# A fused decoder layer: TensorE's instructions in the written order, attention in whole score steps with projections drawn between

## The chip, the cores and the metric

The kernel runs on one core of a Trainium2 chip. The core has five engines that run side by side and wait for each other by semaphores: TensorE (PE; its weight loads are listed apart as PEld), VectorE (DVE), ScalarE (ACT), GpSimd (POOL) and SyncE (SP), which only issues DMAs. The metric is the device time of one execution in microseconds, the median of three runs.

## The reference

One layer of a decoder on 512 positions of width 1024, all in float32:

```
h = rms_norm(x, g_mix);  qa,ka,va,qb,kb,vb,gates = split(h @ w_in)        # 8 + 8 heads of 64
qa, ka = rope(qa), rope(ka)
ya = moba_attention(qa, ka, va)            # softmax over own block of 256 and past blocks, causal
yb = stick_breaking_attention(qb, kb, vb)  # a = sigmoid(z) * prod of (1 - sigmoid(z)) of later keys, causal
g  = sigmoid(gates + b_gate)
x  = x + (g[0] * (ya @ w_branch_a) + g[1] * (yb @ w_branch_b)) @ w_out
h  = rms_norm(x, g_ffn);  u = causal_depthwise_conv(h @ w_up)             # width 3
x  = x + (silu(u_gate) * u_val) @ w_down                                  # d_ff 2816
return rms_norm(x, g_final)
```

With 512 positions and blocks of 256 the three chosen past blocks are all there are, so the MoBA part is plain causal softmax attention.

## The kernel before

All matrix products are made in three passes (`mm3`, line 70): each operand is split into a high and a low half (`whi`, `wlo` for weights, two planes of one tile for activations), and high x high, high x low and low x high are summed in PSUM. A projection is 8 such triples over the depth of 1024 ("8 units" below), 24 TensorE instructions of 512 columns. A weight block of 128 x 1024 is loaded by SP (`raw`, 512 KB), its high half made by ScalarE (line 66) and its low half by VectorE (line 67); three such blocks are held (`wsp`), so a block's halves are made when the block three before is used up.

In the order of the program: the input is loaded transposed in 8 pieces `xk`, scaled by the norm's weight and split (`xg`), while the Q and K columns of the first two pairs of MoBA heads (`qk0`, lines 182 to 185) are summed over them and the sum of squares `ssq` is gathered. `rstd_cols` (line 113) sums `ssq` over the partitions by products with `ones` (line 116) and takes the reciprocal root, `bcast_rows` (line 132) spreads it over the partitions by TensorE transposes (line 135) into `rb`. Then V of the MoBA heads (`vproj_a`), then attention. `moba_half` makes Q or K of a pair: a copy `pc`, its rotated half `sw` by four DMAs on ScalarE's queue, three VectorE products, a split. `sb_qk` makes those of the stick-breaking heads (`o`, then the split), `vproj_b` their V, in products of 256 columns.

`attend(branch, pairs)` (line 331) handles two pairs of heads at a time, in three units of query tiles of 128: tiles 0 and 1, tile 2, tile 3. For each unit: scores into PSUM tile `sc` (two buffers, `psc`), for MoBA with a mask product in front (line 281); the weights (`weights_a`: maximum, exponential, reciprocal, product; `weights_b`: two sigmoids, selects on GpSimd, scans on VectorE, product); transposes of the weights into PSUM tile `tp` (one buffer, `ptr`); the copy `aT` out of it, by VectorE for some MoBA units and by ScalarE for the rest. Then the products with V into `tp` (line 358). Projections use PSUM tile `mm` (two buffers).

After attention come the gates, the two output projections and their sum, `w_out`, a second norm (`norm2`, line 463, with `ssq2`), up-projection with convolution and gate, down-projection and the last norm.

The program is written in this order, but the order on each engine is set by a list scheduler with a model of its own (line 610). It takes what it thinks is ready: so, before, projections are pulled into attention wherever the model sees a gap, `mm` triples are split between scores, and products of later stages run ahead of a waiting one. `tc.issue_after` (line 352) only holds the products with V behind the last transposes.

Of the kernel before, what the change touches and what calls it, by code (L numbers as in the profile page):

```python
# [25 lines left out]
NG = 3  # L26
NWARM = 8
LAST = 4
# [10 lines left out]
def trunk_layer(ctx: ExitStack, tc: tile.TileContext, xT: bass.AP, w: bass.AP, vec: bass.AP,  # L39
# [3 lines left out]
    def pool(stack, name, bufs, space=None, side=None):  # L43
# [40 lines left out]

    warmb = consts.tile([128, 512], BF, name="warmb")
    nc.vector.memset(warmb, 0.0)
# [53 lines left out]

    hlp = pool(asta, "hlp", 2)
    st1 = ExitStack()
# [6 lines left out]
    for _ in range(NWARM):  # L149
        nc.tensor.matmul(warm, warmb[:, :128], warmb, start=True, stop=True)  # L150
    xks = {}
# [36 lines left out]
    def vproj_a():  # L188
        ps = [pool_.tile([128, S], F32, name=n) for pool_, n in ((pmm, "mm"), (pmm, "mm"), (p1, "v0"), (p1, "v1"))]
        for k in range(KT):  # L190
            if k % 2 == 0:
                wt = wload(("va", k // 2))
            for t in range(QT):
                a = (xg[k][:, 0, t * 128:(t + 1) * 128], xg[k][:, 1, t * 128:(t + 1) * 128])
                mm3(ps[t], a, blk(wt, k % 2, 512), k == 0, k == KT - 1)
        for t in range(QT):
            if t % 2:
                nc.scalar.activation(va[:, t], ps[t], AF.Copy, scale=r1[:, t:t + 1])
            else:
                nc.vector.tensor_scalar(va[:, t], ps[t], r1[:, t:t + 1], None, op0=OP.mult)  # L200

    def vproj_b(g):
        wt = tuple(wload(("vb", g, h)) for h in range(2))
        for t in range(QT):
# [3 lines left out]
            for k in range(KT):  # L208
                a = (xg[k][:, 0, t * 128:(t + 1) * 128], xg[k][:, 1, t * 128:(t + 1) * 128])
                mm3(o, a, blk(wt[k // 4], k % 4, 256), k == 0, k == KT - 1)  # L210
            if t % 2:
# [4 lines left out]
    mst = ExitStack()  # L216
    mp = pool(mst, "mp", 1, side="right")
    va = mp.tile([128, QT, 512], F32, name="va")
    rt = pool(mst, "rt", 2, side="right")
    mqkp = pool(mst, "mqkp", 4, side="right")  # L220
    swp = pool(mst, "swp", 2, side="right")
    tg = mp.tile([128, 2, S], F32, name="tg")
    nc.sync.dma_start(tg, trig)
    for i in range(2):
        nc.vector.tensor_mul(tg[:, i], tg[:, i], rb)

    def proj(wt):
        ps = pmm.tile([128, S], F32, name="mm")
        for k in range(KT):
            mm3(ps, blk(wt, k), (xg[k][:, 0], xg[k][:, 1]), k == 0, k == KT - 1)  # L230
        return ps

# [24 lines left out]
    def moba_qk(p):  # L257
        for n in range(2):
            moba_half(p, n, proj(wload(("mqk", p, n))), swp)

    def sb_qk(p):
        sc = {}
        for n, nm in enumerate(("q", "k")):
            ps = proj(wload(("sqk", p, n)))
# [5 lines left out]
            sc[nm] = sqkp.tile([128, 2, S], F32R, name=f"hl{nm}")  # L270
            split_out(sc[nm], o)
        stk["b", p] = [(sc["q"], sc["k"], h * 64) for h in range(2)]

    UNITS = ((0, 1), (2,), (3,))

    def scores(br, p, seg):
        sc = psc.tile([128, 2, 512], F32, name="sc")
        if br == "a":
            for j, (qt, o, n) in enumerate(seg):
                for h in range(2):  # L280
                    nc.tensor.matmul(sc[:, h, o + n - 128:o + n], identb, maskb, start=j == 0, stop=False,
                                     skip_group_check=True)
        for qt, o, n in seg:
            for m, (c, d) in enumerate(((0, 0), (0, 1), (1, 0))):
                for h in range(2):
                    q, k, r0 = stk[br, p][h]
                    nc.tensor.matmul(sc[:, h, o:o + n], q[r0:r0 + 64, c, qt * 128:(qt + 1) * 128],  # L287
                                     k[r0:r0 + 64, d, :n], start=br == "b" and m == 0, stop=m == 2,
                                     skip_group_check=True)
        return sc  # L290

# [38 lines left out]

    def attend(br, pairs):
        v = va if br == "a" else vb
        aT = {p: atp.tile([128, 2, 10 * 128], F32, name="aT") for p in pairs}
        for u, qts in enumerate(UNITS):
            seg = []
            for qt in qts:
                seg.append((qt, sum(s[2] for s in seg), (qt + 1) * 128))
            W = seg[-1][1] + seg[-1][2]
            scs = [scores(br, p, seg) for p in pairs]
            ws = [(weights_a if br == "a" else weights_b)(sc, seg) for sc in scs]  # L340
            for p, a in zip(pairs, ws):
                tp = ptr.tile([128, 2, 512], F32, name="tp")
                for h in range(2):
                    for c in range(0, W, 128):
                        last = nc.tensor.transpose(tp[:, h, c:c + 128], a[:, h, c:c + 128], ident)  # L345
                o = seg[0][0] * (seg[0][0] + 1) // 2 * 128
                if br == "b" or u % 2:
                    nc.scalar.activation(aT[p][:, :, o:o + W], tp[:, :, :W], AF.Copy)
                else:
                    nc.vector.tensor_copy(aT[p][:, :, o:o + W], tp[:, :, :W])  # L350
        av = ptr.tile([128, 2, 512], F32, name="tp")
        with tc.issue_after(last.ins):
            for j, p in enumerate(pairs):
                for qt in range(QT):
                    o = qt * (qt + 1) // 2 * 128
                    for kb in range(qt + 1):
                        for h in range(2):
                            nc.tensor.matmul(av[h * 64:(h + 1) * 64, j, qt * 128:(qt + 1) * 128],  # L358
                                             v[:, kb, (2 * p + h) * 64:(2 * p + h + 1) * 64],
                                             aT[p][:, h, o + kb * 128:o + (kb + 1) * 128],  # L360
                                             start=(kb == 0), stop=(kb == qt))
        for j, p in enumerate(pairs):
# [12 lines left out]
    ptr = pool(psA, "ptr", 1, PSUM)  # L375
    attend("a", (0, 1))
    moba_qk(2)
    moba_qk(3)
    attend("a", (2, 3))
# [4 lines left out]
    sqkp = pool(ysta, "sqkp", 4, side="right")  # L384
    gsig = pool(ysta, "gsig", 6, side="right")
    sb_qk(0)
    sb_qk(1)
    vproj_b(0)
    attend("b", (0, 1))
    sb_qk(2)  # L390
    sb_qk(3)
    vproj_b(1)
    attend("b", (2, 3))

    def gate(i, b):
        ps = proj(wload(("g", i, b)))
        g = gsig.tile([128, S], F32, name="g")
        nc.vector.tensor_mul(g, ps, rb)
        return g

    pend = {}

    def gates(i):
        pend[i] = []
        for b in range(2):
            g = gate(i, b)
            nc.scalar.activation(g, g, AF.Sigmoid, bias=bgate[:, b * 8 + i:b * 8 + i + 1])
            pend[i].append(g)

    gates(0)  # L410
    for i in range(1, NG):
        gates(i)
    psA.close()
# [14 lines left out]
    for i in range(KT):  # L428
        if i >= NG:
            gates(i)  # L430
        wab = wload(("ab", i))
# [182 lines left out]
```

## Time and profile before

| | us |
|---|---|
| median of three runs | 755.24 (755.08 to 755.56) |
| the profiled execution | 755.25 |
| its span, first to last instruction | 752.9 |
| TensorE busy | 742.3 (99%) |
| TensorE weight loads busy | 612.8 (81%) |
| VectorE busy | 446.9 (59%) |
| ScalarE busy | 309.6 (41%) |

The span is what the trace shows; 2.35 us of the execution lie around it. Matrix products overlap by their pipeline, so their single durations (0.39 us for 512 columns) add up to more than the time that they take; the time is read from start to start. The granted clock says which share of full speed TensorE had in a stretch.

### The profile page before, as it was taken

To read this page: it belongs to the slowest core of one execution; us is meant where nothing else is said; L and a number is where in the kernel's file an instruction comes from. 1 tells how busy PE (TensorE), PEld (TensorE's weight loads), DVE (VectorE), ACT (ScalarE), POOL (GpSimd) and SP (SyncE) were. 2 spreads that over 40 slices of the span, in tenths; PEclk is the share of its full clock that TensorE was granted. 3 is DMA by queue.
4 is the path that set the end of the run, shared out by engine and by line. 5 is a ranking of instruction groups with operands and counts; after the bars stand their busy time and mean duration, and the time that the engine had idled before them with its cause. 6 is when DMAs were issued, how large, how long until landed. Compare 5 with 4: busy or idle time off the path is not lost.

```text
span 752.9 us, 9484 instructions
## 1 busy us (share of the span) xinstructions
PE 742.3 (99%) x3792; PEld 612.8 (81%) x3792; DVE 446.9 (59%) x638; ACT 309.6 (41%) x445; POOL 20.4 (3%) x40
## 2 busy tenths in 40 slices
PE   9999998999999999999999999999999999999996
PEld 6887787979878888888888888888888888888885
DVE  6588767684883544446548777767777673122233
ACT  6445526363563323324345444444443442121233
POOL 0000000220310000000000000000000000000000
PEclk9999999999999999999999999999999999999999
DMA  9542211111123423232322323232322223323202
GB/s 311 153 129 84 84 58 57 51 62 57 57 85 123 158 85 111 84 111 85 112 84 84 112 84 112 85 110 86 104 92 95 103 89 108 111 85 102 94 28 111
DMA packets 23899, 74.11 MB, mean 98 GB/s; under 512 B 2992, under 2 KB 3632, under 8 KB 23856
## 3 DMA queue, kind: packets, MB, share of 16 engines
q1 hardware_dynamic: 21456, 70.11, 28.5%
q10 hardware_dynamic: 2400, 3.41, 1.6%
q8 instruction: 29, 0.48, 0.3%
q14 instruction: 14, 0.11, 0.0%
HBM read 69.31 MB, written 2.10 MB: 95 GB/s over the span
## 4 chain that ended last, share of the span: by engine, by line
PE 97%; DVE 1%; DMA 0%; ACT 0%; issue 0%; ACTq 0%
PE mm L71 23%; PE mm L73 23%; PE mm L72 23%; PE d L73 5%; PE d L72 5%; PE d L71 5%; PE q L184 3%; PE sc L287 3%; PE tp L358 2%; PE tp L345 2%; PE v L72 0%; PE v L71 0%; PE v L73 0%; DMA raw<-w 0%; PE d L517 0%; DVE st L296 0%
## 5 line engine op out<-in xcount | busy, mean ns | idle before, releaser
L66 ACT ACTIVATE whi<-raw 128x1024 fp32r<-128x1024 f32 (+2 forms) x128 | 129.8, 1020 | 244.3 <-PE mm L72 88.8
L67 DVE TENSOR_TENSOR wlo<-raw,whi 128x1024 fp32r<-128x1024 f32 (+2 forms) x128 | 149.5, 1173 | 98.7 <-ACT whi L66 97.6
L73 PE MATMUL mm<-h,wlo 128*128 128x512 f32 x352 | 137.1, 390 | 0.0
L72 PE MATMUL mm<-h,whi 128*128 128x512 f32 x352 | 137.0, 389 | 0.0
L71 PE MATMUL mm<-h,whi 128*128 128x512 f32 x352 | 136.9, 389 | 0.0
L71 PE MATMUL mm<-xg,whi 128*128 128x512 f32 x224 | 88.3, 394 | 0.0
L73 PE MATMUL mm<-xg,wlo 128*128 128x512 f32 x224 | 88.2, 394 | 0.0
L72 PE MATMUL mm<-xg,whi 128*128 128x512 f32 x224 | 88.0, 393 | 0.0
L73 PEld LDWEIGHTS mm<-h,wlo 128*128 128x128 f32 x352 | 66.1, 188 | 13.8
L72 PEld LDWEIGHTS mm<-h,whi 128*128 128x128 f32 x352 | 66.1, 188 | 13.7
L71 PEld LDWEIGHTS mm<-h,whi 128*128 128x128 f32 x352 | 66.1, 188 | 13.6
L71 PE MATMUL d<-whi,gT 128*128 128x512 f32 x176 | 68.9, 393 | 0.0
L73 PE MATMUL d<-whi,gT 128*128 128x512 f32 x176 | 68.3, 389 | 0.0
L72 PE MATMUL d<-wlo,gT 128*128 128x512 f32 x176 | 68.3, 389 | 0.0
L490 DVE TENSOR_TENSOR u<-mm,rb 128x512 f32<-128x512 f32 x44 | 30.1, 688 | 37.8 <-PE mm L73 37.7
L71 PEld LDWEIGHTS mm<-xg,whi 128*128 128x128 f32 x224 | 42.1, 188 | 10.4 <-issue 1.7
L73 PEld LDWEIGHTS mm<-xg,wlo 128*128 128x128 f32 x224 | 42.1, 188 | 9.9 <-issue 1.5
L72 PEld LDWEIGHTS mm<-xg,whi 128*128 128x128 f32 x224 | 42.1, 188 | 9.2 <-issue 0.7
L73 PEld LDWEIGHTS d<-whi,gT 128*128 128x128 f32 x176 | 33.0, 188 | 6.8
L72 PEld LDWEIGHTS d<-wlo,gT 128*128 128x128 f32 x176 | 33.1, 188 | 6.6
L71 PEld LDWEIGHTS d<-whi,gT 128*128 128x128 f32 x176 | 33.1, 188 | 6.6
L234 ACT ACTIVATE gT<-t 128x512 fp32r<-128x512 f32 x22 | 13.9, 631 | 55.1 <-DVE t L499 55.1
(184 smaller groups left out, 1047.1 us busy)
## 6 DMA issues: line engine op xcount, KB each, us to landing
raw<-w SPq DMA_DIRECT2D x118, 512.0 KB, 3.3
xk<-xT SPq DMA_DIRECT2D x8, 256.5 KB, 5.3
sw<-pc ACTq DMA_DIRECT2D x32, 64.0 KB, 2.0
x1T<-xT SPq DMA_DIRECT2D x8, 256.0 KB, 5.1
raw<-w SPq DMA_DIRECT2D x6, 256.0 KB, 6.1
out<-on ACTq DMA_DIRECT2D x4, 256.0 KB, 2.7
out<-on SPq DMA_DIRECT2D x4, 256.0 KB, 2.5
tg<-trig SPq DMA_DIRECT2D x1, 512.0 KB, 7.5
```

The costliest lines, as they stand in the source:

```text
L66: nc.scalar.activation(hi[:, sl], raw[:, sl], AF.Copy)
L67: nc.vector.tensor_sub(lo[:, sl], raw[:, sl], hi[:, sl].bitcast(F32))
L71: nc.tensor.matmul(ps, a[0], b[0], start=start, stop=False)
L72: nc.tensor.matmul(ps, a[0], b[1], start=False, stop=False)
L73: nc.tensor.matmul(ps, a[1], b[0], start=False, stop=stop)
L184: nc.tensor.matmul(qk0[c], w0[i][:, (k % 2) * 512 + c * 128:(k % 2) * 512 + (c + 1) * 128], xg[k][:, j], start=(k == 0 and n == 0), stop=( ...
L234: nc.scalar.activation(hl[:, 0], o, AF.Copy)
L287: nc.tensor.matmul(sc[:, h, o:o + n], q[r0:r0 + 64, c, qt * 128:(qt + 1) * 128], k[r0:r0 + 64, d, :n], start=br == "b" and m == 0, stop=m ...
L345: last = nc.tensor.transpose(tp[:, h, c:c + 128], a[:, h, c:c + 128], ident)
L358: nc.tensor.matmul(av[h * 64:(h + 1) * 64, j, qt * 128:(qt + 1) * 128], v[:, kb, (2 * p + h) * 64:(2 * p + h + 1) * 64], aT[p][:, h, o + k ...
L490: nc.vector.tensor_mul(u, ps, rb2)
```

## The change

A line at the top makes TensorE's order that of the program text; the other engines are still ordered by the scheduler. Since nothing is pulled ahead on TensorE now, the text says what stands between the steps of attention. Projections become generators that yield after each triple (1.0 unit, or 0.5 for a triple of 256 columns) and stand in a list `fillers` in the order in which they are needed: Q and K of MoBA pairs 2 and 3, then of stick-breaking pairs 0 and 1, V, and so on to the gates. `attend` is written in steps: scores of unit 0 for both pairs, of unit 1 for both, transposes of unit 0 for the first pair, for the second, scores of unit 2, then the transposes of units 1 and 2, pair by pair. After each step `fill(gap)` draws as many units from the list as `GAPS_*` says. Of the scores, the mask products of both pairs stand first.

```diff
-NWARM = 8
+NWARM = 32
+    ctx.enter_context(tc.manual_schedule(engines={mybir.EngineType.PE}))
-            (eng if eng is not None and i < 2 else nc.sync).dma_start(raw[:, sl], w[WIDX[key]][:, sl])
-            if eng is not None and i == 1:
+            (eng if eng is not None and i == 0 else nc.sync).dma_start(raw[:, sl], w[WIDX[key]][:, sl])
+            if eng is not None and i == 0:
...
-    warmb = consts.tile([128, 512], BF, name="warmb")
+    warmb = consts.tile([128, 128], BF, name="warmb")
...
+    def proj(key, use):
+        wt = wload(key)
+        ps = pmm.tile([128, S], F32, name="mm")
+        for k in range(KT):
+            mm3(ps, blk(wt, k), (xg[k][:, 0], xg[k][:, 1]), k == 0, k == KT - 1)
+            if k < KT - 1:
+                yield 1.0
+        use(ps)
+        yield 1.0
...
+    def fill(n):
+        while n > 0 and fillers:
+            try:
+                n -= next(fillers[0])
+            except StopIteration:
+                fillers.pop(0)
...
-            scs = [scores(br, p, seg) for p in pairs]
-            ws = [(weights_a if br == "a" else weights_b)(sc, seg) for sc in scs]
-            for p, a in zip(pairs, ws):
...
+        steps = [(score, 0), (score, 1)] + [(turn, 0, p) for p in pairs] + [(score, 2)]
+        steps += [(turn, u, p) for u in (1, 2) for p in pairs]
+        for (f, *args), gap in zip(steps, gaps):
+            f(*args)
+            fill(gap)
...
+    fillers = [moba_qk(2), moba_qk(3), sb_qk(0), sb_qk(1), vproj_b(0), sb_qk(2), sb_qk(3), vproj_b(1)]
+    fillers += [gates(i) for i in range(NG)]
+    GAPS_A = (14, 0, 4, 6, 0, 4, 8, 4, 4)
+    GAPS_A2 = (10, 0, 3, 6, 0, 3, 6, 3, 3)
+    GAPS_B = (8, 4, 4, 4, 4, 4, 8, 4, 4)
+    attend("a", (0, 1), GAPS_A)
+    attend("a", (2, 3), GAPS_A2)
...
+    attend("b", (0, 1), GAPS_B)
+    attend("b", (2, 3), GAPS_B)
+    fill(1000)
```

Besides, the stick-breaking Q and K now share the four buffers of the MoBA ones, `vproj_a` takes its PSUM tiles in another order, the first weight block comes with one quarter on ScalarE's queue in place of two, and the warm-up is 32 products of 128 columns in place of 8 of 512.

The order on TensorE in the first MoBA attend, where `sc_651` and `sc_660` are the scores of unit 1 of the two pairs, `tp_635` the transposes of unit 0 of the first pair, and `mm_896` a projection. Before:

```order
L73 MATMUL mm_896<-xg1_99,wlo_892 128x512
...
L287 MATMUL sc_651<-hl1_399,hl0_385 128x384
L345 MATMUL tp_635<-ident_67,a1_610 128x128
L287 MATMUL sc_651<-hl1_399,hl0_385 128x384
L345 MATMUL tp_635<-ident_67,a1_610 128x128 x5
L287 MATMUL sc_651<-hl1_399,hl0_385 128x384 x4
...
L287 MATMUL sc_660<-hl1_427,hl0_413 128x384 x6
L71 MATMUL mm_896<-xg2_100,whi_891 128x512
```

After, with `sc_731` and `sc_732`, `tp_765` and `tp_806` in these places and `mm_712` and `mm_799` for the projections:

```order
L74 MATMUL mm_712<-xg5_105,wlo_708 128x512
...
L307 MATMUL sc_731<-hl1_425,hl0_411 128x384 x6
L307 MATMUL sc_732<-hl1_453,hl0_439 128x384 x6
L375 MATMUL tp_765<-ident_69,a1_636 128x128 x6
L72 MATMUL mm_712<-xg6_106,whi_707 128x512
...
L74 MATMUL mm_799<-xg1_101,wlo_795 128x512
L375 MATMUL tp_806<-ident_69,a1_649 128x128 x6
```

The scores of both pairs stand together, then the first pair's transposes whole, then four triples, then the second pair's.

The order on TensorE at the second norm, where `ssq` is the sum of squares, `n2r` the reciprocal root and the `mm` rows up-projections. Before:

```order
L72 MATMUL mm<-h_3131,whi 128x512
L116 MATMUL tp<-ones,ssq_3136 128x2 x4
L73 MATMUL mm<-h_3131,wlo 128x512
...
L72 MATMUL mm<-h_3133,whi 128x512
L135 MATMUL tp<-ident,n2r 128x128 x4
```

After:

```order
L73 MATMUL mm<-h_3157,whi 128x512
L74 MATMUL mm<-h_3157,wlo 128x512
L117 MATMUL tp<-ones,ssq_3158 128x2 x4
L136 MATMUL tp<-ident,n2r 128x128 x4
L72 MATMUL mm<-h_3150,whi 128x512
```

Before, 30 products stand between the two; now none.

The order on ScalarE in the first stick-breaking attend, where `a1` and `a2` are the two sigmoids of a score tile, `aT` the copies of transposes, and `hlq` (now `hl0`) the split of a projection's result `o`. Before:

```order
L312 ACTIVATE a1_1582<-sc_1568 128x2x384
L66 ACTIVATE whi_1838<-raw_1837 128x1024
L348 ACTIVATE aT_1482<-tp_1552 128x2x384
L314 ACTIVATE a2_1584<-sc_1568 128x2x384
L234 ACTIVATE hlq_1762<-o_1760 128x512
```

After:

```order
L332 ACTIVATE a1_1626<-sc_1600 128x2x384
L67 ACTIVATE whi_1787<-raw_1786 128x1024
L249 ACTIVATE hl0_1647<-o_1645 128x512
L334 ACTIVATE a2_1615<-sc_1599 128x2x384
L378 ACTIVATE aT_1490<-tp_1663 128x2x384
```

The first copy of transposes, `aT_1482` before and `aT_1490` now, has moved behind the split of a projection.

## Rows read from the trace of the kernel before

**Rows 1.** The page, parts 1 and 4: engines' busy time, and the chain's shares.

```profile
PE 742.3 (99%) x3792; PEld 612.8 (81%) x3792; DVE 446.9 (59%) x638; ACT 309.6 (41%) x445; POOL 20.4 (3%) x40
...
PE 97%; DVE 1%; DMA 0%; ACT 0%; issue 0%; ACTq 0%
```

**Rows 2.** Table of stretches: length, busy us (instructions) by engine, clock, DMA.

```profile
core 0: us, PE busy (x) PEld busy (x) DVE busy (x) ACT busy (x) POOL busy (x), PEclk, DMA share, GB/s
56.30:240.50 184.20, 181.54 (x1303) 150.60 (x1302) 124.79 (x198) 91.64 (x160) 19.31 (x32) 0.99 0.22 69
116.00:129.00 13.00, 10.34 (x70) 8.08 (x69) 11.91 (x23) 10.96 (x24) 0.00 (x0) 0.87 0.13 42
400.00:500.00 100.00, 100.00 (x443) 82.81 (x442) 76.93 (x100) 49.28 (x61) 0.00 (x0) 1.00 0.29 95
```

**Rows 3.** Timeline of TensorE, 116 to 130: start, length, line, names [idle before, releaser].

```profile
118.00 0.88 PE L345 MATMUL tp<-ident,a 128*128 128x128 f32 x6 [0.81 <-DVE aT L350]
...
123.07 0.88 PE L345 MATMUL tp<-ident,a 128*128 128x128 f32 x6 [0.90 <-ACT aT L348]
```

**Rows 4.** Chain of waits in order of time: start, length, what (instructions).

```profile
57.95 0.88 PE sc L287 x12
...
65.32 0.37 PE sc L287
...
67.01 0.55 PE sc L287 x4
...
84.39 0.65 PE tp L345 x6
...
109.22 0.72 PE sc L287 x6
...
145.35 1.41 PE sc L287 x18
...
192.63 1.58 PE sc L287 x24
```

**Rows 5.** Timeline of all engines, 0 to 40.

```profile
4.22 0.49 DVE L170 TENSOR_SCALAR xg<-xk 128x512 fp32r<-128x512 f32 x1 [2.25 <-DMA xk<-xT]
...
4.89 1.43 PE L184 MATMUL q<-xg,whi 128*128 128x512 f32 x4
...
5.41 1.43 DVE L67 TENSOR_TENSOR wlo<-raw,whi 128x256 fp32r<-128x256 f32 x4
...
24.41 1.48 DVE L159 TENSOR_TENSOR ssq<-ssq,sq 128x512 f32<-128x512 f32 x2
...
29.31 0.95 PE L116 MATMUL mm<-ones,ssq 128*128 128x2 f32 x8
```

**Rows 6.** Timeline of all engines, 389 to 399, the second norm.

```profile
389.71 1.06 ACT L66 ACTIVATE whi<-raw 128x1024 fp32r<-128x1024 f32 x1 [5.51 <-PE mm L72]
...
389.97 0.95 PE L116 MATMUL tp<-ones,ssq 128*128 128x2 f32 x8
...
390.79 1.28 ACT L123 ACT_TABLE_LOAD   x1
...
390.81 1.23 DVE L67 TENSOR_TENSOR wlo<-raw,whi 128x1024 fp32r<-128x1024 f32 x1 [5.21 <-ACT whi L66]
...
392.14 0.21 ACT L123 ACTIVATE n2s<-n2v 128x4 f32<-128x4 f32 x1
...
392.98 0.16 DVE L129 SCALAR_TENSOR_TENSOR n2r<-n2t,n2r 128x4 f32<-128x4 f32 x1
```

**Rows 7.** Timeline of VectorE, 60 to 160.

```profile
69.24 1.81 DVE L296 TENSOR_REDUCE st<-sc 128x2 f32<-128x768 f32 x2
...
74.74 0.95 DVE L350 COPY aT<-tp 128x768 f32<-128x768 f32 x1
...
81.46 0.69 DVE L249 TENSOR_TENSOR sw<-sw,tg 128x512 f32<-128x512 f32 x1 [2.18 <-DMA sw<-pc]
...
148.59 2.48 DVE L326 TENSOR_TENSOR_SCAN R<-a 128x128 f32<-128x128 f32 x4
...
151.91 1.79 DVE L326 TENSOR_TENSOR_SCAN R<-a 128x384 f32<-128x384 f32 x2
```

More of the change, by code (lines that the diff above doesn't have):

```diff
@@ L149, in trunk_layer @@
     for _ in range(NWARM):
-        nc.tensor.matmul(warm, warmb[:, :128], warmb, start=True, stop=True)
+        nc.tensor.matmul(warm[:, :128], warmb, warmb, start=True, stop=True)
     xks = {}
@@ L200, in vproj_a @@
                 nc.vector.tensor_scalar(va[:, t], ps[t], r1[:, t:t + 1], None, op0=OP.mult)
+    mqkp = pool(ysta, "mqkp", 4, side="right")
+    hlp = pool(ysta, "hlp", 2, side="right")
+    mst = ExitStack()
+    mp = pool(mst, "mp", 1, side="right")
+    va = mp.tile([128, QT, 512], F32, name="va")
+    rt = pool(mst, "rt", 2, side="right")
+    swp = pool(mst, "swp", 2, side="right")
+    tg = mp.tile([128, 2, S], F32, name="tg")
+    nc.sync.dma_start(tg, trig)
+    for i in range(2):
+        nc.vector.tensor_mul(tg[:, i], tg[:, i], rb)
+    def proj(key, use):
[7 more added lines that the diff above has]
+        yield 1.0
     def vproj_b(g):
@@ L214, in vproj_b @@
                 nc.vector.tensor_scalar(dst[:, 1], o, r1[:, t:t + 1], None, op0=OP.mult)
[L216 to L231, printed above, removed]
+            yield 0.5
+    def fill(n):
[4 more added lines that the diff above has]
+                fillers.pop(0)
     def split_out(hl, o):
@@ L269, in sb_qk, with scores @@
                 nc.vector.tensor_mul(o, ps, rb)
-            sc[nm] = sqkp.tile([128, 2, S], F32R, name=f"hl{nm}")
+            sc[nm] = mqkp.tile([128, 2, S], F32R, name=f"hl{n}")
             split_out(sc[nm], o)
+        for n, nm in enumerate(("q", "k")):
+            yield from proj(("sqk", p, n), lambda ps: use(n, nm, ps))
         stk["b", p] = [(sc["q"], sc["k"], h * 64) for h in range(2)]
     UNITS = ((0, 1), (2,), (3,))
-    def scores(br, p, seg):
-        sc = psc.tile([128, 2, 512], F32, name="sc")
+    def scores(br, pairs, seg):
+        scs = [psc.tile([128, 2, 512], F32, name="sc") for _ in pairs]
         if br == "a":
[L279 to L290, printed above, removed]
+            for sc in scs:
+                for j, (qt, o, n) in enumerate(seg):
+                    for h in range(2):
+                        nc.tensor.matmul(sc[:, h, o + n - 128:o + n], identb, maskb, start=j == 0, stop=False,
+                                         skip_group_check=True)
+        for p, sc in zip(pairs, scs):
+            for qt, o, n in seg:
+                for m, (c, d) in enumerate(((0, 0), (0, 1), (1, 0))):
+                    for h in range(2):
+                        q, k, r0 = stk[br, p][h]
+                        nc.tensor.matmul(sc[:, h, o:o + n], q[r0:r0 + 64, c, qt * 128:(qt + 1) * 128],
+                                         k[r0:r0 + 64, d, :n], start=br == "b" and m == 0, stop=m == 2,
+                                         skip_group_check=True)
+        return scs
     def weights_a(sc, seg):
@@ L329, in weights_b, with attend @@
         return be
-    def attend(br, pairs):
+    SEGS = []
+    for qts in UNITS:
+        seg = []
+        for qt in qts:
+            seg.append((qt, sum(s[2] for s in seg), (qt + 1) * 128))
+        SEGS.append(seg)
+    def attend(br, pairs, gaps):
         v = va if br == "a" else vb
         aT = {p: atp.tile([128, 2, 10 * 128], F32, name="aT") for p in pairs}
[L334 to L337, printed above, removed]
-            W = seg[-1][1] + seg[-1][2]
-            scs = [scores(br, p, seg) for p in pairs]
-            ws = [(weights_a if br == "a" else weights_b)(sc, seg) for sc in scs]
-            for p, a in zip(pairs, ws):
[L342 to L350, printed above, removed]
-        av = ptr.tile([128, 2, 512], F32, name="tp")
[L352 to L361, printed above, removed]
@@ new lines, in attend, with score, turn @@
+        ws = {}
+        def score(u):
+            scs = scores(br, pairs, SEGS[u])
+            for p, sc in zip(pairs, scs):
+                ws[u, p] = (weights_a if br == "a" else weights_b)(sc, SEGS[u])
+        def turn(u, p):
+            seg = SEGS[u]
+            W = seg[-1][1] + seg[-1][2]
+            a = ws[u, p]
+            tp = ptr.tile([128, 2, 512], F32, name="tp")
+            for h in range(2):
+                for c in range(0, W, 128):
+                    nc.tensor.transpose(tp[:, h, c:c + 128], a[:, h, c:c + 128], ident)
+            o = seg[0][0] * (seg[0][0] + 1) // 2 * 128
+            if br == "b" or u % 2:
+                nc.scalar.activation(aT[p][:, :, o:o + W], tp[:, :, :W], AF.Copy)
+            else:
+                nc.vector.tensor_copy(aT[p][:, :, o:o + W], tp[:, :, :W])
@@ L375, in trunk_layer, with gates, use @@
     ptr = pool(psA, "ptr", 1, PSUM)
[L376 to L379, printed above, removed]
+    def gates(i):
+        pend[i] = []
+        def use(b, ps):
+            g = gsig.tile([128, S], F32, name="g")
+            nc.vector.tensor_mul(g, ps, rb)
+            nc.scalar.activation(g, g, AF.Sigmoid, bias=bgate[:, b * 8 + i:b * 8 + i + 1])
+            pend[i].append(g)
+        for b in range(2):
+            yield from proj(("g", i, b), lambda ps: use(b, ps))
+    pend = {}
+    fillers = [moba_qk(2), moba_qk(3), sb_qk(0), sb_qk(1), vproj_b(0), sb_qk(2), sb_qk(3), vproj_b(1)]
[5 more added lines that the diff above has]
+    attend("a", (2, 3), GAPS_A2)
     mst.close()
```

46 lines of the change are left out of this document (16 added, 30 removed).

## The prediction

> **What bounds the kernel now.** I read the page first, then the table of stretches, the timeline of TensorE where that table shows a gap, and the chain of waits. The page [rows 1] has TensorE busy for 742.3 of 752.9 us, and 97% of the chain that ended last is its own work. So the time is the sum of TensorE's instructions plus its gaps, and anything off TensorE counts only when TensorE waits for it. The table [rows 2] separates the run that cannot be improved from the one that can: in 400 to 500 us there are 443 matrix products in 100 us, 0.226 us each, and no gap. Attention, from the first score at 56.3 us to the last product with V at 240.5, holds 184.2 us, of which 1303 instructions leave TensorE idle for 2.7. All of that idle time lies in 116 to 129 us, where TensorE is busy for 10.3 of 13.0 us at a granted clock of 0.87. [...] The rows of the gap [rows 3] say why: the transposes at 118.00 wait for VectorE's copy and those at 123.07 for ScalarE's copy of the transposes before them, and the scheduler had no projection left to put between.
>
> [...]
>
> **What the change gains.** Nothing is removed from the work: the order shows 405 wide projection products among the attention before and 402 after, and 192 narrow ones in both. What changes is how often TensorE switches. Before, there are 24 runs of scores, 25 of transposes, 31 of projections; now 12, 24 and 32.
> - The gap of 116 to 129 us gets projections between its steps: 2.7 idle plus 1.7 of clock, 4.4 us.
> - Scores of two pairs of heads run as one. Alone, the 12 scores of the first unit take 0.88 us, and 24 in one run take 1.58, not 1.76; 18 of two units take 1.41, where 0.88 and 0.72 apart make 1.60 [rows 4]. So 0.19 us for each merge, and there are 12 runs fewer: 2.3 us.
> - Before, some groups are broken into each other. From 65.32 to 67.56 us (the first and the last row of that mixture) six scores and six transposes take 2.24 us; whole they take 0.72 and 0.65 [rows 4]. That is 0.87 us in a place of 12 instructions, and the order shows three such places of about that size: I take 2.2 us for the three, the other two being less mixed.
> Together 8.9 us. The lower end is the gap alone, 4.4; the upper, if the masks merge as cheaply as the scores, I put at 10.
>
> **What it costs: TensorE may no longer pass a waiting instruction.** Four places, in the order of the program.
>
> *Sum of squares, first norm.* Before, the products with `ones` stand after projections that were pulled ahead, long after `ssq` is ready: 24.41 + 1.48 = 25.89, used at 29.31 [rows 5]. Now they stand behind seven of eight rounds of Q and K, 84 products. VectorE now forms the first `wlo` quarter (1.43 for four, 0.36 each) before the first `xg` (0.49), so the first product starts some 0.85 later than 4.89; that is hidden by the wait that follows. TensorE would have done 84 products and `ones` at 4.89 + 0.5 + 84 x 0.226 + 0.95 = 25.3. `ssq` comes from ScalarE and VectorE, whose order is the old one here, so `ones` ends at 25.9 + 0.95 = 26.85 at the earliest: 1.5 us lost. The first loads shift by one issue on SP (a quarter of the first weight leaves ScalarE's queue); for that and for the broadcast of the norm, which VectorE now copies behind one more `wlo`, I add 0.3. Total 1.8, between 1.2 and 2.8. The eight warm-up products become 32 of a quarter of the columns: same columns, over before the first data, cost 0.
>
> *Second norm.* The diff does not touch it, but the order does: `ones` and the transposes that need its result now stand next to each other, with nothing between. Before, ScalarE's chain for it (a weight half at 389.71, the table load 1.28, the square root at 392.14) and VectorE's ended at 392.98 + 0.16 = 393.14, 3.43 us after the weight half could start [rows 6], and 30 products covered it. That same weight half waits for the end of the up-projection that now precedes `ones`, so the 3.43 us start there; `ones` itself uses 0.95 of them. TensorE waits 2.5, with the semaphores 2.6. VectorE's `wlo` (1.23) stands in that queue too, beside the table load, and costs nothing. Bounds: 2.3, and 4.3 if the clock falls as it did in the gap (1.7).
>
> *First MoBA attend.* There is one PSUM tile for transposes, so the second pair's transposes wait for the first pair's copy. After the second score step VectorE's queue holds a maximum, the rotated half `sw`, a maximum, a sum and then the copy: 0.9 + 0.6 + 0.9 + 0.6 + 0.9 = 3.9 us [rows 7]. TensorE has 0.72 of scores, 0.65 of transposes and 12 products, 2.7: 4.1. They tie, and the `sw` product can wait for its DMA, as at 81.46, by 2.18. The next copy is ScalarE's, behind exponentials and the DMA issues of the next rotated half, a like tie. I take 0.5 each, 1.0 us, between 0 and 4.6. The second MoBA attend draws Q and K without rotation, hence without DMA, and I find its copies early: 0.
>
> *First stick-breaking attend.* The place is the copy of the first unit's first transposes, ScalarE's row `aT_1490`. Before it on that queue is `hl0_1647`, which needs `o_1645` from VectorE, and this stands behind ten scans, products and a `wlo`: the first scan can start some 3.1 us after the step (a table load of 1.28 and three ScalarE instructions, an estimate), and from there it takes 2.5 + 1.0 + 2.5 + 0.9 + 1.2 + 0.6 + 1.8 + 0.6 = 11.1 us (scans and `wlo` by their rows, the other products at 0.6 for 512 columns) [rows 6, 7], then three ScalarE instructions, 1.9: 16.1. TensorE gets there after 1.6 of scores, 12 half-width and 18 wide products, 5.5, scores again, 1.4, 12 wide products, 2.7, six transposes, 0.65, and 2.7 more: 14.6. Wait 1.5, between 0 and 2.7. The last attend draws gates, whose sigmoid is not in front of the copy: 0.
>
> For the rest, 0.2 for a clock that falls after one of these waits. The load order on SP is otherwise the old one, and the two products per weight leave each load over 5 us against the gapless run's rate. GpSimd's selects change order with their unit, and stay within the 3 us that the projections give.
>
> Sum: 1.8 + 2.6 + 1.0 + 1.5 + 0.2 = 7.1 lost, 8.9 won: -1.8. The profiled execution took 755.25 us (span 752.9, 2.35 around it), the median of the runs is 755.24, so both give **753.4 us**.
>
> **Rivals.**
> 1. *The copies are never late.* Both attends cost 0 and the gain is 9.9: 755.25 - 9.9 + 4.4 = 749.8. For it: VectorE is busy for 125 of attention's 184 us [rows 2] and has room. Against: it serves in order, and a DMA has held it up.
> 2. *Slower: the copy of the first transposes decides.* If in-order VectorE and ScalarE make the second transposes of a unit late by about 2.2 us (the DMA wait of rows 7 is 2.18) at four of the twelve places, that is 8.8 in place of 2.5, and the time 753.4 + 6.3 = 759.7. It turns the change into a loss when these waits pass 8.9 - 4.6 = 4.3 us in all, two such places. For it: one PSUM tile, ties at two places. Against: before, VectorE waited 2.18 and TensorE did not notice.
> 3. *The change does not do what it says:* the gap comes back whole at the border of two attends, since VectorE was busy for 11.9 of its 13 us [rows 2]. 753.4 + 4.4 = 757.8.
> [...]
>
> **Chances.** The forecast 0.43 (its own range 751.5 to 755.5), rival 1 0.24, rival 2 0.26, rival 3 0.05, rival 4 0.02. Within 0.2%, which is about what a measurement of this kernel can tell from no change, is 753.7 to 756.75. Faster than that: a little over half of the forecast's case, rival 1 and rival 4, 0.49; slower: rivals 2 and 3 mostly, 0.27; the same 0.24. The range 748.5 to 760 takes in rival 1 and rival 2.
>
> **What would show it.** A gapless 116 to 129 and 12 score runs prove the gain. In the waits of TensorE I expect `ones` at the first norm for VectorE's `ssq` (0.7, since the later start hides the rest), the transposes of the second norm for VectorE's `n2r` (2.6), and transposes waiting for `aT` from VectorE and ScalarE for 2.5 us in all. It is wrong if these waits together pass 9 us, if the second norm shows under 1 us, or if the score runs cost as much merged as apart.

## The result and the profile after

The changed kernel takes 760.58 us (median of 4 runs, 758.88 to 761.93) where the kernel before takes 755.23 (755.08 to 755.56): a ratio of 1.0069, 95% interval 1.0045 to 1.0093. It is slower; 753.4 was forecast, and 760.58 lies outside the range. The profiled execution took 759.67, with a span of 757.6 us, 4.7 more than before. On the chips of the later runs the kernel before has two levels, 753.2 to 754.1 us in 37 of 72 executions and 754.7 to 756.3 in 35, at mean clocks of mostly 0.998 and 0.996, so that its median moves by up to 1 us with their mix and differences of that size between groups say little.

The page's parts 1 and 4, which answer to [rows 1]:

```profile
PE 738.8 (98%) x3816; PEld 614.7 (81%) x3816; DVE 450.4 (59%) x638; ACT 310.0 (41%) x445; POOL 22.6 (3%) x40
...
PE 73%; issue 20%; DVE 2%; ACT 2%; DMA 1%; POOL 1%; ACTq 0%; POOLq 0%; DVEq 0%
```

TensorE is busy for 3.5 us less in a span that is 4.7 longer: its work became cheaper and its waits grew by more. (The 20% "issue" in the chain is time for which the profile shows no releaser; no reading rests on it.) The table of TensorE's waits (waits for, us in total, times, longest) has them:

```profile
PE tp L375 <- ACT aT L378: 3.9, 3, 2.0
PE tp L136 <- DVE n2r L130: 2.5, 1, 2.5
PE tp L375 <- DVE aT L380: 1.9, 1, 1.9
PE q L184 <- ACT whi L67: 1.1, 1, 1.1
...
PE mm L72 <- DVE g L416: 0.8, 1, 0.8
PE tp L393 <- DVE aT L380: 0.6, 1, 0.6
PE mm L117 <- DVE ssq L159: 0.2, 1, 0.2
```

The table of stretches, as [rows 2]: all of attention, the second MoBA attend in which the gap of [rows 3] lay, and the run without gaps:

```profile
52.90:234.70 181.80, 175.31 (x1300) 148.45 (x1299) 123.84 (x196) 90.31 (x158) 21.49 (x32) 0.99 0.21 68
104.50:143.50 39.00, 38.84 (x330) 34.18 (x328) 26.29 (x47) 17.14 (x44) 0.00 (x0) 1.00 0.15 49
400.00:500.00 100.00, 100.00 (x443) 82.84 (x442) 73.50 (x93) 45.35 (x56) 0.00 (x0) 1.00 0.28 95
```

The gap is gone (38.84 busy of 39.0, clock 1.00), and the run without gaps is what it was. Three stretches make up the 4.7 us, with 0.226 us for each long product that changed places:
- Up to the first score: 52.93, where before 56.34 held 27 more long products, 50.24 without them: +2.7.
- Attention: 181.8 against 184.2, with three long products fewer 183.5: -1.7, where the steps of the forecast give -6.2.
- After it: 757.6 - 234.7 = 522.9; before 512.4, plus 30 products moved there 519.2: +3.7, made up of the second norm 2.5, a wait for `g` 0.8, the rest 0.4.

Where attention loses, the timeline of VectorE shows (start, length, line, names, [idle before, releaser]):

```profile
65.89 0.96 DVE L316 TENSOR_REDUCE st<-sc 128x2 f32<-128x768 f32 x1 [1.26 <-PE sc L307]
68.71 0.69 DVE L264 TENSOR_TENSOR sw<-sw,tg 128x512 f32<-128x512 f32 x1 [1.86 <-DMA sw<-pc]
69.32 0.95 DVE L316 TENSOR_REDUCE st<-sc 128x2 f32<-128x768 f32 x1
70.18 0.68 DVE L265 TENSOR_TENSOR m<-m,sw 128x512 f32<-128x512 f32 x1
70.78 0.95 DVE L380 COPY aT<-tp 128x768 f32<-128x768 f32 x1
```

The first transposes (66.31, 0.88 long) are done by 67.2; their copy starts at 70.78, because the product with `sw` in front of it waits 1.86 us for a DMA, and a maximum and a sum stand between the two. On TensorE the second transposes stand there:

```profile
66.31 0.88 PE L375 MATMUL tp<-ident,a 128*128 128x128 f32 x6
71.79 0.88 PE L375 MATMUL tp<-ident,a 128*128 128x128 f32 x6 [1.87 <-DVE aT L380]
```

It repeats in the next unit on ScalarE's timeline (ACTq are its DMA issues): the copy stands behind the exponentials of the unit after it, these wait for VectorE's maximum, and that is queued behind the next `sw`. First ScalarE's rows, then two of VectorE's:

```profile
79.08 1.80 ACTq L261 DMA_DIRECT2D sw<-pc  x3
82.01 0.69 ACT L320 ACTIVATE a<-sc,st 128x512 f32<-128x512 f32 x1 [2.30 <-DVE st L316]
...
83.35 0.81 ACT L378 ACTIVATE aT<-tp 128x768 f32<-128x768 f32 x1
```

```profile
77.62 0.69 DVE L264 TENSOR_TENSOR sw<-sw,tg 128x512 f32<-128x512 f32 x1 [1.11 <-DMA sw<-pc]
...
80.70 1.22 DVE L316 TENSOR_REDUCE st<-sc 128x2 f32<-128x1024 f32 x1
```

The transposes of this copy begin at 78.53; the next ones wait 2.04 us for it and start at 84.21. Behind that wait the granted clock falls (columns as in the table of stretches):

```profile
80.00:90.00 10.00, 7.96 (x32) 6.31 (x31) 7.51 (x14) 5.56 (x12) 0.00 (x0) 0.83 0.25 72
84.44:87.86 3.42, 3.42 (x12) 2.91 (x11) 2.68 (x8) 2.36 (x6) 0.00 (x0) 0.50 0.00 0
```

The mean of 0.83 over 10 us comes from 3.4 us at 0.50. In these the long products start every 0.43 us (at 85.79, 86.22, 86.65), behind them every 0.23 (88.36, 88.59, 88.82): about half of the 3.4, 1.7, is lost.

### The profile page after: what moved, and what is told of

Its sections match the earlier page's. It is cut to its first block, busy times and chain, and to the rows that moved or that the text cites. A ratio compares the mean times of both kernels' runs of the same rounds, so it can differ in the third digit from the quotient of the medians.

```text
span 757.6 us, 9539 instructions
## 1 busy us (share of the span) xinstructions
PE 738.8 (98%) x3816; PEld 614.7 (81%) x3816; DVE 450.4 (59%) x638; ACT 310.0 (41%) x445; POOL 22.6 (3%) x40
## 4 chain that ended last, share of the span: by engine, by line
PE 73%; issue 20%; DVE 2%; ACT 2%; DMA 1%; POOL 1%; ACTq 0%; POOLq 0%; DVEq 0%
PE mm L72 18%; PE mm L73 18%; PE mm L74 18%; PE d L74 5%; PE d L72 5%; PE d L73 5%; PE q L184 3%; POOL a L338 1%; DMA sw<-pc 1%; DVE R L346 1%; PE tp L393 1%; ACT whi L67 1%; DMA raw<-w 0%; PE d L544 0%; PE tp L375 0%
## 5 line engine op out<-in xcount | busy, mean ns | idle before, releaser
L72 PE MATMUL mm<-xg,whi 128*128 128x512 f32 x224 | 90.4, 403 | 0.0
L73 PE MATMUL mm<-xg,whi 128*128 128x512 f32 x224 | 87.9, 392 | 0.0
```

The source lines that it names most:

```text
L72: nc.tensor.matmul(ps, a[0], b[0], start=start, stop=False)
L73: nc.tensor.matmul(ps, a[0], b[1], start=False, stop=False)
```

## Experiments

Each kernel is the changed one with the edit shown (the two that begin with "and" build on the one ahead of them), timed against the kernel before on its own chip; times are compared by that ratio (the kernel before took 753.95 to 755.01 there). The first four ran together, the next four, then three, then one.

**The second norm taken apart.**

```diff
-    norm2()
+    r2 = rstd_cols(ssq2, ptr, "tp", "n2")
     ups.append(up_mm())
+    bcast_rows(r2, ptr, "tp", rb2)
```

> The kernel after (760.6 us) with its second norm taken apart: the products with `ones`, then one up-projection of 24 products, then the transposes that spread the result; nothing else changes. Theory: the 2.5 us that TensorE waits for VectorE's `n2r` exist only because nothing stands between the two. 24 products are 5.4 us against the chain of 3.4, so the wait goes to 0 and the time falls by 2.5, to 758.1. Rival: the chain of the norm is delayed by the weight halves of the up-projection that stands in between, ScalarE and VectorE serve those first, and most of the wait stays: 760 or more.

755.35 us, ratio 1.0013 (1.0001 to 1.0024). The wait for `n2r` is gone from the list, so the rival falls. The gain, 0.0056 or 4.2 us against 1.0069, is more than the 2.5 of the wait, but the two intervals together leave over 2 us open. The stretch 380 to 400 shows what can come with the wait: in a second profile of the changed kernel, and in this one,

```profile
380.00:400.00 20.00, 17.55 (x77) 14.59 (x77) 9.36 (x17) 8.99 (x11) 0.00 (x0) 0.91 0.22 78
```

```profile
380.00:400.00 20.00, 20.00 (x95) 16.66 (x95) 10.51 (x18) 7.60 (x10) 0.00 (x0) 1.00 0.27 96
```

A mean of 0.91 over 20 us is 1.8 us of the full clock lost; in the first profile the clock there was 1.00 after the same wait. So the wait costs 2.5, or 4.3 where the clock falls behind it.

**The rotation's DMAs left out.**

```diff
+            if p < 2:
                 nc.scalar.dma_start(sw[r:r + 32], pc[r ^ 32:(r ^ 32) + 32])
-        nc.vector.tensor_mul(sw, sw, tg[:, 1])
+        nc.vector.tensor_mul(sw, sw if p < 2 else pc, tg[:, 1])
```

> The kernel after with the DMAs of the rotated half left out for pairs 2 and 3 (the four halves made during the first MoBA attend): the product with the sines reads `pc` in place of the moved `sw`, so the rotation of these two pairs is not computed. VectorE and ScalarE keep the same instructions, 16 DMA issues on ScalarE's queue go. Theory 1 (a DMA that VectorE waits for in order stands in front of the copy of the transposes): the products and transposes of the first MoBA attend lose 6.5 to 7 us beyond their rate now, of which 4 to 5 go, 756 us. Rival 2 (the maxima, exponentials and copies themselves take longer than the projections between them): over 4.5 us stay, 759 or more.

This kernel leaves out the rotation of pairs 2 and 3. 753.38 us, ratio 0.998 (0.9968 to 0.9992): 6.7 us less than the changed kernel by the ratios, more than the 4 to 5 expected. The first MoBA attend has no wait for a copy left; what remains is 1.7 in the first stick-breaking attend and 0.2 in the second MoBA one:

```profile
PE tp L376 <- ACT aT L379: 1.9, 2, 1.7
```

Attention takes 175.45 us, 6.3 less. Theory 1 holds, and what the first attend loses by these DMAs is 6.3, idle time and clock together. The edit takes away their landing and ScalarE's 16 issues at once; the runs on other queues below tell these apart in part.

**The projections dealt out otherwise.** `GAPS_A = (12, 0, 10, 2, 0, 8, 4, 4, 4)`.

> The kernel after with the 44 projection triples of the first MoBA attend dealt out otherwise: (12, 0, 10, 2, 0, 8, 4, 4, 4) in place of (14, 0, 4, 6, 0, 4, 8, 4, 4), so that 30 products stand behind the first transposes of unit 0 and 24 behind those of unit 1, where 12 stand now. Theory 1: the two waits of 2 us each lie behind these, the copies do not move, and the waits go with the clock that they cost: 4 us less, 756.5. Rival 2: VectorE and ScalarE have no time to spare in this stretch, the wait turns up behind the later transposes: 759 or more, with the waits of the first attend still over 4 us.

756.78 us, ratio 1.0027 (1.0014 to 1.0041). By the ratios 3.2 us less than the changed kernel, half of each theory: the waits behind the first transposes of units 0 and 1 are gone, and a longer one stands behind the second of unit 1 (2.6 in the list of waits). More projections cover one late copy; the lateness stays in the queues.

**The rotation's product and sum on GpSimd.**

```diff
+        e = nc.vector if p < 2 else nc.gpsimd
-        nc.vector.tensor_mul(sw, sw, tg[:, 1])
-        nc.vector.tensor_add(m1, m1, sw)
+        e.tensor_mul(sw, sw, tg[:, 1])
+        e.tensor_add(m1, m1, sw)
```

> The kernel after with two instructions of each of the four later rotations (the product of the moved half with the sines, and the sum) on GpSimd, which has nothing to do in the first MoBA attend; the DMAs stay. VectorE loses 8 instructions (5.5 us) and, by theory 1, the waits for DMA in front of its copies: the copies of unit 0 come 2 us earlier or more, time 756. Rival 2 (the maxima and exponentials are what is late): under 2 us less, 759 or more. A third outcome: the product and the sum are so slow on GpSimd (over 3 us together) that the scores of pairs 2 and 3 or the last half wait for them; then the waits move to the second attend.

759.57 us, ratio 1.0071 (1.0058 to 1.0084): nothing gained. GpSimd takes 1.28 and 1.30 for what VectorE does in 0.69 (the instructions at 76.20 and 77.56), and its wait for the DMA is handed on: the split on ScalarE now waits 4.01 us for `m`, with the exponentials and the copy of unit 1 behind it. Unit 0 has no wait, unit 1 one of 3.5. Moving the waiting instruction is not enough if an in-order queue then waits for its result.

```profile
78.89 0.63 ACT L249 ACTIVATE hl<-m 128x512 fp32r<-128x512 f32 x1 [4.01 <-POOL m L266]
```

**The changed kernel again.**

> The kernel after, unchanged, on the chip of the three that follow, so that they have a common base and the spread of its runs is seen. Expected: 1.0069 times before, as on the first chip, between 1.0045 and 1.0093. Theory: its runs differ by 3 us because the first 84 products of Q and K take 19.6 us in some runs and 21.2 in others (the two sizes seen so far); the rest of the program repeats.

759.08 us, ratio 1.0072 (1.0055 to 1.0088), as expected. Its profile has the first 84 products (up to `ones`, the wait for `ssq` included) in 19.85 us, not 21.2, and 1.8 us lost by the clock behind the second norm. So the expectation names one of two things that vary. The first products in the two profiles:

```profile
5.77 3.73 PE L184 MATMUL q<-xg,whi 128*128 128x512 f32 x8 [1.13 <-ACT whi L67]
```

```profile
5.78 2.06 PE L184 MATMUL q<-xg,whi 128*128 128x512 f32 x8 [1.13 <-ACT whi L67]
```

The same wait stands ahead of both, and the table of stretches gives a clock of 1.00 for both. The trace's clock records tell more: they begin, at the full level, at 9.35 us in the first profile, where the eight slow products end, and at 5.35 in the second, ahead of its first product. For the time before them there is no record, and the table counts it as full. The 13 profiles of changed kernels agree: the first eight products take 3.7 to 3.8 us in the four whose records begin at 9.35 to 10.34, and 2.1 to 2.5 in the nine whose records begin at 3.7 to 5.4. So the products that took long ran ahead of the first record, at 0.44 us each, about half the rate of 0.226, as at the clock of 0.50 in the first attend (0.43). Why the full clock comes later in some executions is not shown.

**The start.** Two quarters of the first weight on ScalarE's queue, as before; `ones` behind the last round of Q and K; 12 products of V ahead of `bcast_rows`.

```diff
-            (eng if eng is not None and i == 0 else nc.sync).dma_start(...)
+            (eng if eng is not None and i < 2 else nc.sync).dma_start(...)
...
-            r1 = rstd_cols(ssq, pmm, "mm", "n1")      # before the products of k = 7
+    r1 = rstd_cols(ssq, pmm, "mm", "n1")              # behind them
```

> The kernel after with two edits of its start taken back or replaced: two quarters of the first weight leave ScalarE's queue again, and the products with `ones` stand behind the last round of Q and K, with 12 products of V between them and the transposes that spread the norm. Theory: the first product comes 0.9 earlier, at 4.9, without a pause after the warm-up, so that the first products run at 0.226 and not at 0.44; nothing waits for `ssq`; the first score falls from 52.9 to about 50.4 and the time by 1.5 (against runs with the fast first products) to 2.6 (against the others). Rival: the first products are slow whatever stands ahead of them, and the wait for `ssq` (25.9 at the earliest) takes back what the earlier start gives: under 1 us.

758.12 us, ratio 1.0048 (1.0035 to 1.0061), 1.8 less than the run above by the ratios, with overlapping intervals. The wait for `ssq` is gone, and the first score stands at 50.78, against 52.93 and 51.60 in the first and the second profile of the changed kernel: 0.8 less than in the second profile, where 1.5 was expected, and 2.2 less than in the first. The pause is shorter (0.69) and not gone; and it is not what makes the first products slow, for they are fast behind 1.13 in the run above and slow behind 0.55 in a later run with this start (the list of the first attend, below).

**The rotation's DMAs on SyncE.**

```diff
-            nc.scalar.dma_start(sw[r:r + 32], pc[r ^ 32:(r ^ 32) + 32])
+            (nc.scalar if p < 2 else nc.sync).dma_start(...)
```

> The kernel after with the 16 DMAs of the rotated halves of pairs 2 and 3 issued on SyncE's queue and not on ScalarE's; the rotation is computed in full. Without these DMAs the first attend lost its waits. Theory A (their issue occupies ScalarE, four take 2.4 us, during which exponentials and copies stand): ScalarE is free, its waits go; VectorE still waits for the landing, 2 us after the issue: the time falls by 3 to 5. Theory B (only the time until landing counts, and it is the same from another queue): under 1.5 us. Third outcome: the weight loads behind these DMAs on SyncE come late, and TensorE waits for `whi`: slower than after.

756.29 us, ratio 1.0022 (1.0011 to 1.0033): 3.8 less than the changed kernel by the ratios, as theory A has it. But theory B's premise fails too: the landing is not the same from another queue. In the kernel after, a weight block is issued on SyncE between the second and the third of the four; the DMA lines of the view by tile (issues with their first and last start, then the time from issue to landing): first this block, then the four `sw` on ScalarE's queue in the kernel after, then the four in the run on SyncE:

```profile
L62 SPq DMA_DIRECT2D raw<-w x1: 328/328/328, 64.1 to 64.1; - x1
...
DMA to landing us min/median/max: 4.1/4.1/4.1
```

```profile
L261 ACTq DMA_DIRECT2D sw<-pc x4: 515/610/612, 63.1 to 64.9; - x4
...
DMA to landing us min/median/max: 2.0/2.9/4.0
```

```profile
L261 SPq DMA_DIRECT2D sw<-pc x4: 577/584/589, 61.8 to 63.7; - x4
...
DMA to landing us min/median/max: 2.0/2.0/2.0
```

The block lands at 68.2. Of the four `sw` on ScalarE's queue, the two issued before it land after 2.0 us, the two issued behind it, at 64.3 and 64.9, after 4.0 and 3.7, at 68.3 and 68.6: with the block. In the kernel after, all eight `sw` DMAs of these pairs that were issued from 0.2 us ahead of a block's issue to 1.1 behind it landed within 0.6 us behind the block, although they hold 64 KB and the block 512. On SyncE's queue the four stand ahead of the next block and take 1.9 to 2.0. Unit 0 still waits 1.1; unit 1 has no wait here, and the copy comes ahead of the exponentials:

```profile
77.38 0.81 ACT L378 ACTIVATE aT<-tp 128x768 f32<-128x768 f32 x1 [0.74 <-PE tp L375]
78.88 0.69 ACT L320 ACTIVATE a<-sc,st 128x512 f32<-128x512 f32 x1 [0.69 <-DVE st L316]
```

The two late `sw` land 0.2 and 0.5 us behind the block. In the trace's packet records their data move late too: the block's from 65.2 to 67.3, theirs from 66.8 and 67.1 on. What makes the delay is not shown.

**The changed text, ordered by the scheduler.** The line with `manual_schedule` left out.

> The kernel after without the line that keeps TensorE's order: the same program, with merged scores and projections dealt out by the same lists, but the scheduler may move TensorE's instructions again. Theory: what is lost is lost by keeping the order (a waiting transpose stops TensorE), so the waits of the first attend and of the second norm shrink to under 3 us together, and the time is 752 to 755. Rival: the scheduler breaks the score runs and uses up the projections early, the gap of the second attend returns (4.4), and the time is that of before or more, 755 to 759.

754.81 us, ratio 1.0008 (1.0 to 1.0017). Both are half right. No wait for a copy or for `n2r` is in the list of waits, which supports that these waits come from keeping the order. But scores run in 34 pieces where the changed kernel has 12, TensorE is busy for 743.2 us and not 738.8, so the gain of whole groups is gone too.

**Four places mended together:** the second norm, the start, SyncE, and for the wait for `g` the two PSUM pools behind attention in the other order.

```diff
-    pmm = pool(psB, "pmm2", 6, PSUM)
     ptr = pool(psB, "ptr2", 2, PSUM)
+    pmm = pool(psB, "pmm2", 6, PSUM)
```

> The kernel after with the four places mended that the runs named: second norm apart (first run), DMAs of the rotated halves on SyncE, the start of the run on it, and the two PSUM pools of the gates' stage swapped, so that its first products do not write the bank that VectorE still reads (the wait for `g`, 0.8). All of it is computed. Theory (the causes are separate and their sizes add): from 759.1 on this chip 2.5 to 4.3 + 4.6 + 1.0 + 0.8 go, 748.5 to 750.5 us, 0.993 to 0.996 of before. Rival: the mended places share their cost (each wait only hides another that is next), and the sum is under 6 us: 753 or more, no faster than before.

748.56 us, ratio 0.9922 (0.9909 to 0.9936). The parts add: by the ratios 11 us less than the changed kernel, where the single runs have 4.2, 3.8 and 1.8 and the wait for `g`, which was not mended alone, 0.8 in the trace. The list of waits has no `n2r`, no `g`, no `ssq`.

**And the list of the first attend.** `GAPS_A = (14, 0, 8, 4, 0, 4, 6, 4, 4)`.

> The kernel of the run before it, and the first attend's list of projections as (14, 0, 8, 4, 0, 4, 6, 4, 4): 24 products behind the first transposes of unit 0, where the DMA on SyncE left a wait of 1.1. Theory: that wait goes and none comes, 1.3 less than the run before it. Rival: the wait moves to unit 1, as when the list was dealt out otherwise with the DMAs on ScalarE: within 0.5 of the run before it.

749.2 us, ratio 0.9933 (0.9919 to 0.9947): not told apart from the run before it. As the rival says, unit 0's wait of 1.1 goes and waits of 0.5 for a copy of ScalarE's and 0.6 for one of VectorE's come later in the attend.

**And the order of the fillers.** `vproj_b(1)` ahead of `sb_qk(2)`, with (8, 6, 6, 4, 4, 6, 8, 5, 5) in the first stick-breaking attend.

> The kernel of the run before it, with the second half of the V projection drawn ahead of Q and K of pairs 2 and 3 in the first stick-breaking attend, and 6 more triples there, (8, 6, 6, 4, 4, 6, 8, 5, 5). Theory: the copy `aT` on ScalarE is late there (2.0 us) because a split of Q waits in front of it for VectorE; the V projection has no such split, so the wait goes: 2 us less than the run before it, about 747. Rival: it is late because of VectorE's scans and whatever is drawn: the wait stays or moves, within 0.7 of the run before it.

747.47 us, ratio 0.9912 (0.9897 to 0.9927). The waits for ScalarE's copies:

```profile
PE tp L385 <- ACT aT L388: 0.6, 2, 0.5
```

They were 2.3 in the run before it. The edit also puts more projections there, so the copy itself must tell; the first copy of the attend in the run before it, then here:

```profile
152.97 0.63 ACT L259 ACTIVATE hl<-o 128x512 fp32r<-128x512 f32 x1 [3.25 <-DVE o L292]
...
154.20 0.80 ACT L388 ACTIVATE aT<-tp 128x768 f32<-128x768 f32 x1
```

```profile
150.24 0.82 ACT L344 ACTIVATE a<-sc 128x768 f32<-128x768 f32 x1 [3.06 <-PE tp L385]
150.95 0.81 ACT L388 ACTIVATE aT<-tp 128x768 f32<-128x768 f32 x1
```

It started 4.4 us after its transposes began (149.78) and starts 1.6 after them here (149.38), with no split in front. This version has the lowest median, 1.6 us less than the last by the ratios and 6.6 less than the kernel before; its interval overlaps with those of the two runs before it.

**The rotation's DMAs on GpSimd's queue.** As on SyncE, with `nc.gpsimd`.

> The kernel after with the 16 DMAs of the rotated halves of pairs 2 and 3 issued on GpSimd's queue: ScalarE is free of their issue, as in the run with SyncE, but they still run beside the weight loads of 512 KB that SyncE issues, where SyncE's own queue puts them ahead of these. It tells apart what the run on SyncE changed twice. Theory L (the landing counts: what is issued beside a weight load lands with it): VectorE waits 1 to 2 us for `sw` in front of the copy of unit 0 as in the kernel after, the transposes there wait about 1.9, and at most 1.5 us of the 2.8 come. Theory I (ScalarE's time for the issue counts): the waits shrink as on SyncE, 2.5 to 4.5 us less than after. Third outcome: the issue on GpSimd is itself much slower than 0.6 us, then the waits grow and it tells nothing of L and I.

754.56 us, ratio 1.0006 (0.9994 to 1.0018): 4.8 to 5.0 us less than the changed kernel by the ratios, a little more than theory I has, while the landing is as theory L has it. Neither alone explains it. VectorE still waits for the landing in unit 0, until 69.3, behind the block that lands at 68.6:

```profile
66.38 1.82 DVE L316 TENSOR_REDUCE st<-sc 128x2 f32<-128x768 f32 x2 [1.25 <-PE sc L307]
69.33 0.69 DVE L264 TENSOR_TENSOR sw<-sw,tg 128x512 f32<-128x512 f32 x1 [1.13 <-DMA sw<-pc]
69.94 0.95 DVE L380 COPY aT<-tp 128x768 f32<-128x768 f32 x1
```

But the order of VectorE changed with the edit: both maxima now stand ahead of `sw` and the copy right behind it, so TensorE waits 0.5 and not 1.9; in unit 1 ScalarE's copy comes ahead of the exponentials and nothing waits. So three things make the loss: a DMA that lands late, its place in VectorE's order, and ScalarE's order with the issues in it. How much ScalarE's time for the issues costs beside its order stays open.

## Why the prediction was wrong

- **The step that failed is the first MoBA attend:** "They tie", "I take 0.5 each, 1.0 us, between 0 and 4.6". It measured 6.3 us (181.8 against 175.45 without the DMAs): waits for copies of 1.9, 2.0 and 0.6, 4.5 together, and 1.7 for the clock that falls behind them, where the sum had 0.2 for the clock in all. The mechanism was in the step, VectorE's `sw` waiting for its DMA in front of the copy; I took the 2.18 us of [rows 7] for a chance event, where in these traces it comes whenever the DMA is issued beside a weight block, and I set the tie at half a microsecond without it. The trace of before shows that already: the `sw` of that row was issued 0.5 us behind a block and landed 0.3 us behind it, 3.9 after its issue. With 6.3 in place of 1.0 the sum is +3.5, not -1.8; the places below bring it to the 4.7 of the span.
- **A place that I did not name:** the first products behind the gates wait 0.8 us for `g`, since they write the PSUM bank that VectorE still reads: with the two pools in the other order (four places mended) the list has no such wait. Nothing may now be put in front of them.
- *Second norm*, forecast 2.6: 2.46 in the trace, 4.3 where the clock falls, as the bounds had it. The rows that answer to [rows 6]:

```profile
389.62 0.95 PE L117 MATMUL tp<-ones,ssq 128*128 128x2 f32 x8
393.03 0.65 PE L136 MATMUL tp<-ident,n2r 128*128 128x128 f32 x4 [2.46 <-DVE n2r L130]
```

- *First norm and start*, forecast 1.8: 2.7 and 1.4 in the two profiles. The forecast had no term for first products at half the rate: in the first profile the eight take 1.7 us longer, `ones` comes later and waits 0.2; in the second it waits 0.6, near the 0.7 forecast.
- *First stick-breaking attend*, forecast 1.5: 1.7, for the reason given (the split of Q in front of the copy, and gone with it in the run with the other order). *Second MoBA attend and last attend*: one wait of 0.2 and none, as forecast.
- *The gains*, forecast 8.9, at most 10: right in sum, with its three terms not measured one by one. The 1.7 of clock in the gap's 4.4 (and in the 4.3 of the second norm) is half of the 3.4 us in which the trace of before has the clock at 0.50:

```profile
124.88:128.29 3.41, 3.39 (x19) 3.17 (x20) 3.30 (x9) 3.39 (x8) 0.00 (x0) 0.50 0.01 2
```

The gap is gone, and scores of two pairs take 1.58 us:

```profile
53.48 1.64 PE L307 MATMUL sc<-hl,hl 64*128 64x128 f32 x24
55.06 0.50 PE L72 MATMUL mm<-xg,whi 128*128 128x512 f32 x1
```

Without the DMAs attention takes 175.45 us with 1.9 of waits left, where 183.5 would be the content of before: 9.9 us won.
- *Rival 2* was nearest: copies late by about 2 us, 759.7. Three places, not four, with 5.8 us of such waits in all, over its border of 4.3; that its number is the profiled 759.67 is luck, since the clock, the wait for `g` and the slow first products make up for the copies' waits that it has too much, 8.8. My own test (all waits together over 9 us) stands at its edge: 2.5 + 5.8 + 0.2 = 8.5, and 9.1 with the 0.6 of the products with V, which the forecast did not list. I put it second because before, VectorE waited 2.18 "and TensorE did not notice". That was evidence about a TensorE that could pass the waiting instruction, and the change takes just this away. Rivals 1 and 3 fell: copies were late, and the gap did not return. Nor was a wait made up later, to which the chances give 0.02 as rival 4: behind the 2.46 us for `n2r` the products start 0.22 us apart or more (393.43, 393.75, 393.97, 394.20, 394.44), and mended waits came back as time.

## What to carry to other kernels

When an engine loses the right to pass a waiting instruction, every wait that the trace of before shows on another engine ahead of it must be priced in full, also those that cost nothing so far, as the 2.18 us for `sw` here. Keep groups whole and in the written order where nothing waits, and give each wait something to stand behind: here four small edits (a norm taken apart, a DMA in front of a large load and not beside it, a PSUM bank not reused at once, a later sum of squares) turn 0.7% lost into 0.8% won; a fifth, with 0.9%, takes a wait of 1.7 us out of the trace, but the times do not tell it apart.

## What the runs showed of the hardware

- In the kernel after, a 64 KB DMA issued on another queue from 0.2 us ahead of a 512 KB load to 1.1 behind it landed with the load, after 3.6 to 5.1 us, where the others took 1.9 to 2.1; ahead of the load on the same queue (the DMAs on SyncE) it took 1.9 to 2.0.
- After the same idle 2.5 us TensorE's clock fell in the second profile of the changed kernel (0.91 in the stretch of 20 us) and not in the first (1.00).
- The first eight products take 3.7 us in the first profile of the changed kernel and 2.1 in the second; those at 3.7 ran before the trace's first clock record (at 9.35 us; 5.35 in the other), and the table of stretches reads 1.00 for both.
- An element-wise product or sum of 128 x 512 took 1.27 to 1.33 us on GpSimd (the run with the rotation on it, four instructions from 76.20 to 83.00) and 0.68 or 0.69 on VectorE in the kernel after.
